# Down projections of two SwiGLU FFNs as Strassen pairs in a hybrid decoder layer

## Chip, core and metric

The kernel runs on one core of a Trainium2 chip. The metric is the device time of one execution in microseconds (us). Three executions of the kernel before took 1840.78, 1842.61 and 1845.76 us, median 1842.61. TensorE is called PE, VectorE DVE, ScalarE ACT, GpSimd POOL and SyncE SP; PEld is PE's loading of the stationary operand.

## Reference

One decoder layer on 256 tokens of width 2048, in float32. Two SwiGLU FFNs with inner width 5632 stand around a mixer; a gated per-layer embedding and a norm end it. Cut to what matters here:

```
def swiglu(x, w_gate, w_up, w_down):
    return (jax.nn.silu(x @ w_gate) * (x @ w_up)) @ w_down

h = h + 0.5 * swiglu(rms_norm(h, norm_ffn1[i]), w1_gate[i], w1_up[i], w1_down[i])
z = rms_norm(h, norm_mix[i]) @ w_in[i]
...            # s5 state space group, gMLP group, norms
h = h + y @ w_out[i]
h = h + 0.5 * swiglu(rms_norm(h, norm_ffn2[i]), w2_gate[i], w2_up[i], w2_down[i])
gate = jax.nn.sigmoid(rms_norm(h, norm_ple[i]) @ w_ple_gate[i])
h = h + gate * (p[i] @ w_ple_proj[i])
```

## The kernel before

**Three passes.** Every product keeps float32 accuracy by splitting each operand into a rounded high part and a rest: wh by ACT (L201) and wl by DVE (L202) for the weights, and the same for the 128x128 stationary blocks of activations. Each product is three matmuls of 512 columns: high times wh, high times wl, low times wh (L207 to L209).

**One stream.** The planner writes a list of steps, and `stream` runs it as one sequence of *subs*. A load brings 4 k rows of 512 columns of a weight (1 MB) into one of four buffers, three of `raw` and one of `xraw`. A sub takes two of the four k rows: one split on ACT and one on DVE, then 12 matmuls (2 k rows, 2 token halves, 3 passes). At sub i the splits up to sub i + 3 have been issued (`LA_SPLIT` = 3, four buffers of wh and wl). What belongs to a finished group of products (its `post`) is a generator, resumed some subs later, as many as it yields. All engines take their instructions in the order in which the program writes them, so a post stands in DVE's and ACT's queues behind the splits already issued.

**FFN.** The 5632 inner columns are 11 blocks c of 512. Gate and up of a block are 16 k rows each, 4 steps. In the second FFN blocks 1 to 10 are a `Pair`: gate and up run side by side, and the first of the four steps ("SNNN") is in Strassen's form: seven products P1, Q5, P2, P6, Q4, P7, P3 of 6 matmuls each, 42 instead of 48, with DVE sums s1 to s4 of the weights (L165) and sums of the transposed h made once (`sums_of_h`). P1, Q5, P6 and P7 have banks of PSUM of their own (`aux`), the others go straight into the four result banks C0 to C3 (`acc`); `aux_post` adds the own banks up afterwards. An ordinary step N has 4 subs, two of each weight.

**Turning g.** The product g = silu(gate) * up of a block is needed with its inner columns on partitions. `flip` transposes 32x32 squares on DVE (L492), writes the block to DRAM on POOL's queue and `fetch` reads it back in four transfers (L505); then ACT and DVE split it. In the first FFN all eleven blocks of g stay in SBUF as high and low parts (`gTa`, `gTb`); in the second, blocks 0 to 4 are kept in DRAM until gate and up are through.

**Down.** Four groups n of 512 result columns, one after another, each over 44 k rows (11 steps). The post of group n adds half of the result to h (L626, two DVE operations), takes squares for the next norm on ACT (L323), and turns the block of h for the next stage: n = 0 to 2 by `flip`, n = 3 by PE transposes (L299).

The functions that the change touches follow.

Of the kernel before, what the change touches and what calls it, by code (L numbers as in the profile page):

```python
# [15 lines left out]
P = 128  # L16
# [5 lines left out]
NW = 512  # L22
# [26 lines left out]
def steps_of(which, c):  # L49

    return "SNNN" if which == 2 and c > 0 else None
# [15 lines left out]
class Pair:  # L67


    ORDER = ("P1", "Q5", "P2", "P6", "Q4", "P7", "P3")  # L70
    BANK = {"P2": "C0", "Q4": "C1", "P3": "C2"}

    def __init__(self, layer, gate, up, steps, post):
        self.layer, self.groups, self.steps, self.post = layer, (gate, up), steps, post
        gate.pair = up.pair = self
        self.banks = {}
# [15 lines left out]
class Layer:  # L92
# [38 lines left out]
    def stream(self):  # L131
        nc = self.nc
        subs, loads = [], []
# [14 lines left out]
        raws, split, sums = {}, {}, {}  # L148
        paired = [i for i, e in enumerate(loads) if e[0].pair]
        p0, p1 = paired[0], paired[-1]  # L150
        state = {"ld": 0, "sp": 0}

        def load(li):
# [3 lines left out]
            pool = self.pools["xraw"] if p0 <= li <= p1 and (li - p0) % 4 == 3 else self.raw_p  # L157
# [24 lines left out]
        def do_split():  # L182
# [4 lines left out]
            if li >= p0 and ahead < p1:  # L187
# [42 lines left out]
        for i in range(n):  # L230
            ahead = i + LA_SPLIT + 1
# [5 lines left out]
            if isinstance(g, Pair):  # L237
                wh, wl = split.pop(i)
                name = g.ORDER[s0]
                for j in range(2):  # L240
                    into(g.bank(name), self.act_S(name, k0, j), wh[:, j], wl[:, j])
# [83 lines left out]
    def h_to_T(self, n, gcol, flip):  # L325

        if flip:
# [11 lines left out]
            if gcol == 32:  # L339
                yield from self.sums_of_h(n, tr)  # L340
# [14 lines left out]
    def sums_of_h(self, n, tr):  # L355

        nc = self.nc
        if n == 0:
            self.S = [self.pools["qt"].tile([P, BW], F32R, tag="qt", name=f"S{x}") for x in "hl"]
        st = self.pools["yss"].tile([P, 1024], F32, tag="st", name="st")  # L360
        a = tr.rearrange("p (i t kk u) -> p t kk i u", i=4, t=2, kk=4)
        a11, a12, a21, a22 = (a[:, t, k:k + 2] for t in range(2) for k in (0, 2))
        s1, s2, s3, s4 = (st[:, 256 * m:256 * m + 256].rearrange("p (kk i u) -> p kk i u", kk=2, i=4) for m in range(4))
        for o, x, y, op in ((s1, a21, a22, ALU.subtract), (s2, s1, a11, ALU.subtract), (s3, a11, a21, ALU.subtract),
                            (s4, a12, s2, ALU.add)):
            nc.vector.tensor_tensor(out=o, in0=x, in1=y, op=op)
        sh, sl = (x[:, 512 * n:512 * n + 1024] for x in self.S)
        yield 1
        self.split_plain(st, sh, sl)

# [3 lines left out]
    def kernel(self):  # L374
# [24 lines left out]
        self.gsk = [dram.tile([P, 4 * 256], F32, name=f"gsk{c}") for c in range(self.KA[1])]  # L399
# [14 lines left out]
        self.open_g(1)  # L414
        self.open("gs", "gs")
# [49 lines left out]


    KA = 6, 5

    def open_g(self, which):
        n = self.KA[which - 1]  # L470
        self.open("gta", "gt")
        self.gT_a = [self.pools["gta"].tile([P, n, 4 * 256], F32R, name=f"gTa{x}") for x in "hl"]

    def open_gb(self, which):
        self.open("gtb", "gtb")
        n = 11 - self.KA[which - 1]
        self.gT_b = [self.pools["gtb"].tile([P, n, 4 * 256], F32R, name=f"gTb{x}") for x in "hl"]

    def gT_at(self, which, c):
        n = self.KA[which - 1]  # L480
        if c < n:
            return self.gT_a, c
        return self.gT_b, c - n
# [23 lines left out]
    def ffn_groups(self, which):  # L507
# [5 lines left out]
        def gate_post(c):  # L513
            def post(g):
                if which == 2 and c == 0:
                    self.close_mix()
                    self.open_gb(2)
                    self.open("gs", "gs")
                    self.open("sums", "sums", 3)
                    self.open("xraw", "xraw")  # L520
# [8 lines left out]
        def up_post(c):  # L529
            def post(g):  # L530
                gt = st.pop(c)
                if which == 1 and c == 6:
                    self.close("wrk")
                    self.open_gb(1)
# [3 lines left out]
                yield from turn(c, gt)  # L538
            return post

        def split_g(c, tr):
            (th, tl), k = self.gT_at(which, c)
            self.split_plain(tr.rearrange("p (i b u) -> p b i u", i=4, b=8),
                             th[:, k, :].rearrange("p (b i u) -> p b i u", b=8, i=4),
                             tl[:, k, :].rearrange("p (b i u) -> p b i u", b=8, i=4))

        def turn(c, gt):
            if which == 2 and c < self.KA[1]:
                self.flip(gt, c)
                return  # L550
            tr = self.flip(gt)
            if which == 1 or c < 10:
                yield 6
                split_g(c, tr)
                return

            for x in ("xraw", "sums", "gs", "qt"):
                self.close(x)
            self.open_g(2)
            self.open("land", "land")  # L560
            land = self.pools["land"].tile([P, 4 * 256], F32, name="land")
            self.fetch(self.gsk[0], land)
            yield 6
            split_g(c, tr)
            split_g(0, land)
            self.fetch(self.gsk[1], tr)
            self.fetch(self.gsk[2], land)
            yield 4
            split_g(1, tr)
            self.fetch(self.gsk[3], tr)  # L570
            yield 1
            split_g(2, land)
# [766 lines left out]
```

## Time and profile before

| what | value |
|---|---|
| median of three executions | 1842.61 us |
| profiled execution | 1842.27 us, its span 1840.3 us |
| PE busy | 1827.1 us, 8452 matmuls |
| DVE busy, ACT busy | 1266.1 us, 891.9 us |
| splits of weights on DVE (L202) | 639 operations, 782.1 us |
| DMA | 405.11 MB, mean 220 GB/s |

A row of the timeline gives the start and the duration of an instruction in us, its engine, line, operation, output and inputs, and in brackets how long the engine stood idle before it and what released it. A matmul's duration is longer than the distance to the next one, since matmuls overlap; the distance between starts is what counts. The same holds, by less, for DVE operations that follow each other closely ("x2" in a row: two of them, with the time of both). A row by form gives count, busy time in all and the mean in ns of one operation.

### The profile page before, as it was taken

How to read it: one execution, taken by the hardware profiler on the slowest of the kernel's cores; microseconds unless marked ns; L12 is line 12 of the kernel's file. 1: busy time of each engine (PE TensorE's matmuls, PEld its weight loads, DVE VectorE, ACT ScalarE, POOL GpSimd, SP SyncE). 2: the span in 40 equal slices, each digit the busy share in tenths (PEclk: the TensorE clock that was granted, in tenths of full speed). 3: DMA queues.
4: the chain of work that ended last, by engine and by line, in shares of the span. 5: the costliest groups of instructions: out<-in, count | busy, mean ns of one | idle time of the engine just before them, and what ended most of it. 6: DMA issues, size and time to landing. Idle time of an engine off the chain costs nothing.

```text
span 1840.3 us, 22012 instructions
## 1 busy us (share of the span) xinstructions
PE 1827.1 (99%) x8452; PEld 1513.8 (82%) x8452; DVE 1266.1 (69%) x1701; ACT 891.9 (48%) x1054; POOL 132.3 (7%) x208
## 2 busy tenths in 40 slices
PE   9999999999999999999999999999999999999998
PEld 7888888888888888888888888888888888888887
DVE  6788886555545554688877678888888856455565
ACT  7444444444444444445446645555555545444454
POOL 1000000000000000022200000000000012000000
PEclk9999999999999999999999999999999999999999
DMA  8667777666666655566545665555666667566553
GB/s 329 225 243 264 241 262 252 225 211 224 223 208 209 223 211 195 223 246 223 181 177 189 225 235 199 195 216 197 232 235 226 222 217 258 197 222 212 193 203 136
DMA packets 72617, 405.11 MB, mean 220 GB/s; under 512 B 10176, under 2 KB 15552, under 8 KB 29888
## 3 DMA queue, kind: packets, MB, share of 16 engines
q1 hardware_dynamic: 62000, 371.67, 56.5%
q0 software_dynamic: 10080, 31.47, 5.7%
q8 instruction: 66, 1.08, 0.2%
q10 hardware_dynamic: 432, 0.57, 0.1%
q14 instruction: 39, 0.32, 0.0%
HBM read 376.28 MB, written 27.26 MB: 219 GB/s over the span
## 4 chain that ended last, share of the span: by engine, by line
PE 94%; DMA 2%; DVE 2%; issue 1%; ACT 1%; POOL 0%; SPq 0%; POOLq 0%; DVEq 0%; ACTq 0%
PE acc L207 23%; PE acc L209 23%; PE acc L208 23%; PE C L207 7%; PE C L209 7%; PE C L208 7%; DMA tr<-gsc 1%; PE P L208 1%; PE y L968 1%; PE P L209 1%; PE P L207 1%; DMA raw<-in_w_gate 1%; PE tr L299 1%; PE v L921 0%; DVE wl L202 0%
## 5 line engine op out<-in xcount | busy, mean ns | idle before, releaser
L202 DVE TENSOR_TENSOR wl<-raw,wh 128x1024 fp32r<-128x1024 f32 (+1 forms) x639 | 782.1, 1234 | 483.9 <-ACT wh L201 481.7
L201 ACT ACTIVATE wh<-raw 128x1024 fp32r<-128x1024 f32 (+1 forms) x639 | 674.4, 1058 | 709.4 <-PE acc L209 536.3
L207 PE MATMUL acc<-wh,hTh 128*128 128x512 f32 (+1 forms) x1104 | 432.0, 391 | 0.2 <-ACT wh L201 0.2
L208 PE MATMUL acc<-wl,hTh 128*128 128x512 f32 (+1 forms) x1104 | 429.3, 389 | 1.5 <-DVE wl L202 1.5
L209 PE MATMUL acc<-wh,hTl 128*128 128x512 f32 (+1 forms) x1104 | 429.2, 389 | 0.0
L208 PEld LDWEIGHTS acc<-wl,hTh 128*128 128x128 f32 x1104 | 207.4, 188 | 44.9 <-DVE wl L202 3.0
L207 PEld LDWEIGHTS acc<-wh,hTh 128*128 128x128 f32 x1104 | 207.3, 188 | 43.3 <-ACT wh L201 0.6
L209 PEld LDWEIGHTS acc<-wh,hTl 128*128 128x128 f32 x1104 | 207.3, 188 | 42.9
L207 PE MATMUL C<-wh,hTh 128*128 128x512 f32 x520 | 202.5, 389 | 0.0
L209 PE MATMUL C<-wh,hTl 128*128 128x512 f32 x520 | 202.5, 389 | 0.0
L208 PE MATMUL C<-wl,hTh 128*128 128x512 f32 x520 | 202.3, 389 | 0.0
L207 PE MATMUL acc<-wh,gTbh 128*128 128x512 f32 x352 | 137.1, 389 | 0.6 <-ACT gTbh L303 0.6
L209 PE MATMUL acc<-wh,gTbl 128*128 128x512 f32 x352 | 137.0, 389 | 0.5 <-DVE gTbl L304 0.5
L208 PE MATMUL acc<-wl,gTbh 128*128 128x512 f32 x352 | 136.9, 389 | 0.0
L207 PE MATMUL acc<-wh,gTah 128*128 128x512 f32 x352 | 136.9, 389 | 0.0
L208 PE MATMUL acc<-wl,gTah 128*128 128x512 f32 x352 | 136.9, 389 | 0.0
L209 PE MATMUL acc<-wh,gTal 128*128 128x512 f32 x352 | 136.9, 389 | 0.0
L209 PEld LDWEIGHTS C<-wh,hTl 128*128 128x128 f32 x520 | 97.6, 188 | 20.5
L208 PEld LDWEIGHTS C<-wl,hTh 128*128 128x128 f32 x520 | 97.6, 188 | 20.5
L207 PEld LDWEIGHTS C<-wh,hTh 128*128 128x128 f32 x520 | 97.6, 188 | 20.3
L498 POOL DMA_DIRECT2D gsc<-tr x25 | 14.2, 569 | 927.5 <-DVE tr L492 927.5
L207 PEld LDWEIGHTS acc<-wh,gTbh 128*128 128x128 f32 x352 | 66.1, 188 | 14.7 <-ACT gTbh L303 1.0
(288 smaller groups left out, 1841.4 us busy)
## 6 DMA issues: line engine op xcount, KB each, us to landing
raw<-in_w_up SPq DMA_DIRECT2D x88, 1024.0 KB, 5.8
raw<-in_w_down SPq DMA_DIRECT2D x88, 1024.0 KB, 4.8
raw<-in_w_gate SPq DMA_DIRECT2D x86, 1024.0 KB, 4.9
raw<-in_w_in SPq DMA_DIRECT2D x24, 1024.0 KB, 4.8
raw<-in_w_out SPq DMA_DIRECT2D x16, 1024.0 KB, 4.8
raw<-in_w_ple_gate SPq DMA_DIRECT2D x16, 1024.0 KB, 4.8
gsc<-tr POOLq DMA_DIRECT2D x25, 512.0 KB, 3.2
tr<-gsc POOLq DMA_DIRECT2D x100, 128.0 KB, 5.5
```

The lines of the kernel that those rows point to most:

```text
L201: nc.scalar.activation(out=wh[:, 0:nk, :], in_=src, func=AF.Copy)
L202: nc.vector.tensor_tensor(out=wl[:, 0:nk, :], in0=src, in1=wh[:, 0:nk, :].bitcast(F32), op=ALU.subtract)
L207: nc.tensor.matmul(o, a[0], wh, start=first, stop=False)
L208: nc.tensor.matmul(o, a[0], wl, start=False, stop=False)
L209: nc.tensor.matmul(o, a[1], wh, start=False, stop=last)
L299: self.nc.tensor.transpose(ps[:, i * P:(i + 1) * P], b, self.ident)
L498: nc.gpsimd.dma_start(out=sc, in_=tr)
L968: nc.tensor.matmul(ps[:, 64 * i:64 * i + 64], R[ri][:, i, :], qt[:, f0:f0 + 64], start=False, stop=(a == 1 and ri == 1))
```

## The change

- The four down groups become two pairs (columns 0 to 1023 and 1024 to 2047). Each pair goes over the 11 blocks of g with the steps `DOWN = "NSNNSNNSNNN"`, so 3 of 11 are in Strassen's form. The own banks are added up by `Pair.post` (the former `aux_post`), and `Pair.finish` adds that to each result bank before the post goes on.
- g of all eleven blocks, in both FFNs, is written to DRAM (`gsk`) and not fetched at once. In the down products `fetch(i)` brings block i into one of two `land` buffers, and `split_g(i)` splits it into one of three `stat` buffers one step ahead; for an S step it makes the four sums of that block and splits them too. As there are two pairs, each block is fetched and split twice per FFN. These calls stand in the plan as "do" entries at the start of each step.
- Blocks 8, 9 and 10 of the first FFN become gate/up pairs "SNNN"; the sums of the transposed h for them are made at block 6 (`sums_of_hT`).
- In both FFNs two more buffers of wh and wl (`ex`) let the splits run five subs ahead instead of three.
- Block n = 2 of h is turned by PE transposes, as n = 3 was; block n = 1 is turned six subs later than its group's end.

```diff
-    return "SNNN" if which == 2 and c > 0 else None
+    return "SNNN" if c > (7 if which == 1 else 0) else None
+DOWN = "NSNNSNNSNNN"
...
+    def finish(self, g, t):
+        i = self.groups.index(g)
+        x = self.rest[i][t]
+        self.layer.nc.vector.tensor_tensor(out=x, in0=g.ps[t], in1=x, op=ALU.subtract if i and t else ALU.add)
+        return x
...
+            if e[0] == "do":
+                at.setdefault(len(subs), []).append(e[1])
+                continue
...
-                wh = self.wh_p.tile([P, KS, NW], F32R, tag="wh", name="wh")
-                wl = self.wl_p.tile([P, KS, NW], F32R, tag="wl", name="wl")
+                ps = self.wh_p, self.wl_p
+                home[i] = self.ex_on > 0 and sum(not home[j] for j in split if j in home) > LA_SPLIT
+                if home[i]:
+                    ps = (self.pools["ex"],) * 2
+                wh = ps[0].tile([P, KS, NW], F32R, tag="wh", name="wh")
+                wl = ps[1].tile([P, KS, NW], F32R, tag="wl", name="wl")
...
-            ahead = i + LA_SPLIT + 1
+            for f in at.pop(i, ()):
+                f()
+            ahead = i + LA_SPLIT + 1 + self.ex_on
...
+        def fetch(i):
+            if i < 22:
+                land[i] = self.pools["land"].tile([P, 4 * 256], F32, tag="land", name="land")
+                self.fetch(self.gsk[i % 11], land[i])
+        def split_g(i):
+            if i == 22:
+                return
+            tr = land.pop(i)
+            stat[i] = [self.pools["stat"].tile([P, 4 * 256], F32R, tag=x, name=x) for x in ("gTh", "gTl")]
+            self.split_plain(tr.rearrange("p (i b u) -> p b i u", i=4, b=8),
+                             *(x.rearrange("p (b i u) -> p b i u", b=8, i=4) for x in stat[i]))
+            if DOWN[i % 11] == "S":
+                ss[i] = [self.pools["ss"].tile([P, 4 * 256], F32R, tag=x, name=x) for x in ("gSh", "gSl")]
+                st = self.pools["sums"].tile([P, 4 * 256], F32, tag="sum", name="st")
+                self.sums_of_T(tr.rearrange("p (i t kk u) -> p t kk i u", i=4, t=2, kk=4), st, *ss[i])
+        def at_step(i):
+            def f():
...
+                split_g(i + 1)
+                fetch(i + 3)
+            return f
...
+            for j in range(11):
+                self.plan += [("do", at_step(11 * p + j))] + pair.plan(j)
...
+        def down_post(n, pair):
             def post(g):
                 for t in range(2):
+                    x = pair.finish(g, t)
                     hs = self.h[:, t, n * NW:(n + 1) * NW]
                     self.nc.vector.scalar_tensor_tensor(
-                        out=hs, in0=g.ps[t], scalar=0.5, in1=hs, op0=ALU.mult, op1=ALU.add)
+                        out=hs, in0=x, scalar=0.5, in1=hs, op0=ALU.mult, op1=ALU.add)
...
-                yield from self.h_to_T(n, 16 if which == 1 else 48, n < 3)
+                if n == 1:
+                    yield 6
+                yield from self.h_to_T(n, 16 if which == 1 else 48, n < 2)
```

Three places of the order that the prediction speaks of, all in the first FFN (the second has the same). Place A is DVE's queue at the first S step after gate/up; g and z, y are the gate and up results, C their banks, s the weight sums, st the sums of a block of g. Before, the down products follow the last block of gate/up like this:

```order
L492 STREAM_TRANSPOSE tr<-g_3926 128x4x4x32
L492 STREAM_TRANSPOSE tr<-g_3927 128x4x4x32
L202 TENSOR_TENSOR wl<-raw,wh 128x1024 x6
L304 TENSOR_TENSOR gTbl<-tr,gTbh 128x1024
L202 TENSOR_TENSOR wl<-raw,wh 128x1024 x16
```

Now the end of the last gate/up pair and the first S step of the down products share the stretch:

```order
L248 TENSOR_TENSOR wl<-s_4142,wh 128x1024
L107 TENSOR_TENSOR y<-C_3914,y 128x512
L107 TENSOR_TENSOR z<-C_3973,z 128x512
L207 TENSOR_TENSOR s_4204<-s_4182,raw 128x1024
L248 TENSOR_TENSOR wl<-raw,wh 128x1024
L207 TENSOR_TENSOR s_4224<-raw 128x1024
L248 TENSOR_TENSOR wl<-s_4182,wh 128x1024
L603 SCALAR_TENSOR_TENSOR g_3942<-y,r_95,g_3942 128x512
L603 SCALAR_TENSOR_TENSOR g_3943<-z,r_95,g_3943 128x512
L542 STREAM_TRANSPOSE tr<-g_3942 128x4x4x32
L542 STREAM_TRANSPOSE tr<-g_3943 128x4x4x32
L248 TENSOR_TENSOR wl<-s_4204,wh 128x1024
```

The finish of the pair (L107), its products (L603) and transposes (L542) now stand between the splits of the S step's factors.

Place B is DVE's queue where the second half of the down products begins; before, that is between the groups n = 1 and n = 2:

```order
L626 SCALAR_TENSOR_TENSOR h<-acc_4472,h 128x512
L626 SCALAR_TENSOR_TENSOR h<-acc_4473,h 128x512
L492 STREAM_TRANSPOSE tr<-h 128x4x4x32 x2
L202 TENSOR_TENSOR wl<-raw,wh 128x1024 x6
L338 TENSOR_TENSOR hTl<-tr,hTh 128x4x128 x2
```

Now, from the end of the first pair on to the first S step's Q5:

```order
L107 TENSOR_TENSOR y<-C_4230,y 128x512
L675 SCALAR_TENSOR_TENSOR h<-y,h 128x512
L107 TENSOR_TENSOR z<-C_4231,z 128x512
L675 SCALAR_TENSOR_TENSOR h<-z,h 128x512
L352 TENSOR_TENSOR gTl<-land,gTh 128x1024
L411 TENSOR_TENSOR st<-land 128x256
L411 TENSOR_TENSOR st<-st,land 128x256
L411 TENSOR_TENSOR st<-land 128x256
L411 TENSOR_TENSOR st<-land,st 128x256
L352 TENSOR_TENSOR gSl<-st,gSh 128x1024
L207 TENSOR_TENSOR s_5145<-s_5101,raw 128x1024
L248 TENSOR_TENSOR wl<-s_5101,wh 128x1024
```

Two operations per result block became four, and the split of g with its sums stands behind them, ahead of the second factor's split.

Place C is DVE's queue at the end of the FFN, where h of the last block is made for PE's transposes. Before:

```order
L202 TENSOR_TENSOR wl<-raw,wh 128x1024 x16
L626 SCALAR_TENSOR_TENSOR h<-acc_5266,h 128x512
L626 SCALAR_TENSOR_TENSOR h<-acc_5267,h 128x512
L288 TENSOR_TENSOR rs<-ssq_102 128x2
L290 TENSOR_TENSOR rs<-rs,ssq_102 128x2 x2
```

Now:

```order
L248 TENSOR_TENSOR wl<-raw,wh 128x1024
L365 SCALAR_TENSOR_TENSOR hTl<-tr,gcol,hTh 128x256 x2
L248 TENSOR_TENSOR wl<-raw,wh 128x1024
L365 SCALAR_TENSOR_TENSOR hTl<-tr,gcol,hTh 128x256 x2
L107 TENSOR_TENSOR y<-C_5191,y 128x512
L675 SCALAR_TENSOR_TENSOR h<-y,h 128x512
L107 TENSOR_TENSOR z<-C_5192,z 128x512
L675 SCALAR_TENSOR_TENSOR h<-z,h 128x512
```

The operations that make h stand behind those that split the turned block n = 2 (hTl), which wait for ACT and for PE's transposes of that block.

## Rows read from the trace of the kernel before

**Rows 1.** Page, busy time, share of the span and instructions of each engine

```profile
PE 1827.1 (99%) x8452; PEld 1513.8 (82%) x8452; DVE 1266.1 (69%) x1701; ACT 891.9 (48%) x1054; POOL 132.3 (7%) x208
```

**Rows 2.** Waits of PE: line, what it waited for, us in total, times, longest

```profile
PE acc L208 <- DVE wl L202: 1.5, 3, 0.8
...
PE acc L207 <- ACT gTbh L303: 0.6, 1, 0.6
PE acc L209 <- DVE gTbl L304: 0.5, 1, 0.5
...
PE P L208 <- DVE wl L202: 0.2, 1, 0.2
```

**Rows 3.** Window of one gate/up pair in the second FFN

```profile
core 0: us, PE busy (x) PEld busy (x) DVE busy (x) ACT busy (x) POOL busy (x), PEclk, DMA share, GB/s
1110.52:1152.95 42.43, 42.43 (x187) 34.85 (x187) 34.31 (x36) 21.89 (x22) 0.55 (x1) 1.00 0.59 210
```

**Rows 4.** Timeline of PE: plain subs, then one Strassen step (42 matmuls from 1108.99)

```profile
1105.59 0.39 PE L207 MATMUL C<-wh,hTh 128*128 128x512 f32 x1
...
1108.31 0.39 PE L207 MATMUL C<-wh,hTh 128*128 128x512 f32 x1
...
1108.99 0.39 PE L207 MATMUL P<-wh,hTh 128*128 128x512 f32 x1
...
1118.75 0.40 PE L207 MATMUL C<-wh,hTh 128*128 128x512 f32 x1
```

**Rows 5.** Chain of waits: start us, us, what; FFN ends

```profile
739.09 0.44 PE tr L299 x4
...
1510.01 7.48 DMA tr<-gsc
```

**Rows 6.** Groups of instructions by form

```profile
L202 DVE TENSOR_TENSOR wl<-raw,wh 128x1024 fp32r<-128x1024 f32 x637 | 780.7, 1236 | 481.5 <-ACT wh L201 479.3
...
L165 DVE TENSOR_TENSOR s<-raw 128x1024 f32<-128x1024 f32 x20 | 24.3, 1216 | 0.0
L323 ACT ACTIVATE junk<-h 128x512 f32<-128x512 f32 x38 | 24.0, 631 | 31.4 <-DVE h L626 15.1 <-DVE h L1109 8.9 <-DVE h L1214 6.9
...
L303 ACT ACTIVATE gTah<-tr 128x1024 fp32r<-128x1024 f32 x8 | 8.4, 1054 | 7.4 <-DMA tr<-gsc 7.4
...
L323 ACT ACTIVATION_READ_ACCUMULATOR junk<-h 128x1 f32 x38 | 7.1, 186 | 0.0
```

**Rows 7.** Timeline of DVE around one Strassen step, operations close together

```profile
1109.07 1.22 DVE L202 TENSOR_TENSOR wl<-raw,wh 128x1024 fp32r<-128x1024 f32 x1 [0.62 <-ACT wh L201]
1110.21 1.22 DVE L165 TENSOR_TENSOR s<-raw 128x1024 f32<-128x1024 f32 x1
...
1113.62 0.68 DVE L605 TENSOR_TENSOR y<-C,y 128x512 f32<-128x512 f32 x1
1114.22 0.68 DVE L605 TENSOR_TENSOR z<-C,z 128x512 f32<-128x512 f32 x1
...
1119.36 0.74 DVE L609 SCALAR_TENSOR_TENSOR g<-y,r,g 128x512 f32<-128x512 f32 x1
...
1120.68 1.29 DVE L492 STREAM_TRANSPOSE tr<-g 128x512 f32<-128x512 f32 x2
1121.90 2.31 DVE L202 TENSOR_TENSOR wl<-raw,wh 128x1024 fp32r<-128x1024 f32 x2
...
1124.14 0.68 DVE L588 TENSOR_TENSOR g<-P,g 128x512 f32<-128x512 f32 x1
1124.85 0.69 DVE L589 TENSOR_TENSOR y<-Q,g 128x512 f32<-128x512 f32 x1
```

**Rows 8.** Timeline of DVE, four sums of a stationary, first and next operation

```profile
1006.83 0.42 DVE L366 TENSOR_TENSOR st<-tr 128x256 f32<-128x256 f32 x1
...
1008.30 0.87 DVE L317 SCALAR_TENSOR_TENSOR hTl<-tr,gcol,hTh 128x256 fp32r<-128x256 f32 x2
```

**Rows 9.** Page, DMA issues: KB each, median us from issue to landing

```profile
raw<-in_w_down SPq DMA_DIRECT2D x88, 1024.0 KB, 4.8
...
tr<-gsc POOLq DMA_DIRECT2D x100, 128.0 KB, 5.5
```

More of the change, by code (lines that the diff above doesn't have):

```diff
@@ L147, in stream @@
         n_tail = sum(sb[0] is tail for sb in subs)
-        raws, split, sums = {}, {}, {}
-        paired = [i for i, e in enumerate(loads) if e[0].pair]
-        p0, p1 = paired[0], paired[-1]
+        raws, split, sums, home = {}, {}, {}, {}
+        run = {}
+        i = 0
+        while i < len(loads):
+            j = i
+            while j < len(loads) and loads[j][0].pair:
+                j += 1
+            for x in range(i, j):
+                run[x] = i, j - 1
+            i = j + 1
         state = {"ld": 0, "sp": 0}
@@ L156, in load @@
             g, k0, nk = loads[li]
-            pool = self.pools["xraw"] if p0 <= li <= p1 and (li - p0) % 4 == 3 else self.raw_p
+            pool = self.pools["xraw"] if li in run and (li - run[li][0]) % 4 == 3 else self.raw_p
             t = pool.tile([P, KL, NW], F32, tag="raw", name="raw")
@@ L186, in do_split @@
             ahead = li + (3 if isinstance(g, Pair) and s0 > 2 else 2)
-            if li >= p0 and ahead < p1:
+            if li in run and ahead < run[li][1]:
                 ahead += 1
@@ L547, in turn @@
[L547 to L572, printed above, removed]
-            self.fetch(self.gsk[4], land)
-            yield 3
-            split_g(3, tr)
-            yield 1
-            split_g(4, land)
@@ L579, in pair_of @@
[L579 to L592 removed]
+                self.flip(gt, c)
@@ L602, in up_end @@
                 yield 1
-                for t, op in enumerate((ALU.add, ALU.subtract)):
-                    x = m["u"][t]
-                    self.nc.vector.tensor_tensor(out=x, in0=g.ps[t], in1=x, op=op)
+                us = [pair.finish(g, t) for t in range(2)]
                 yield 2
+                gt = pair.rest[0]
                 for t in range(2):
-                    x = m["g"][t]
-                    self.nc.vector.scalar_tensor_tensor(out=x, in0=m["u"][t], scalar=r[:, t:t + 1], in1=x,
+                    self.nc.vector.scalar_tensor_tensor(out=gt[t], in0=us[t], scalar=r[:, t:t + 1], in1=gt[t],
@@ L610, in up_end @@
                                                         op0=ALU.mult, op1=ALU.mult)
-                yield from turn(c, m["g"])
+                self.flip(gt, c)
             gate.post, up.post = gate_end, up_end
-            pair = Pair(self, gate, up, steps_of(which, c), aux_post)
-            for j, x in enumerate(pair.steps):
-                self.plan += [("S", pair, 4 * j)] if x == "S" else [(gate, 4 * j, 4), (up, 4 * j, 4)]
-        def act_g(k, t):
-            x, c = self.gT_at(which, k // 4)
+            pair = Pair(self, gate, up, steps_of(which, c), self.act_S)
@@ L646, in ffn_groups @@
                 self.whole(up)
-        first = 0 if which == 1 else self.KA[1]
-        for n in range(4):
-            g = Group(wd, n * NW, 44, act_g, down_post(n))
-            self.plan += [(g, 4 * (c % 11), 4) for c in range(first, first + 11)]
+        for p in range(2):
+            down_pair(p)
     def vexp(self, pool, x, out):
@@ L1263, in final_post @@
             yield 1
-        tail = self.plan[-1][0]
-        last = tail.post
+        before = self.plan[-1][0]
+        last = before.post
         def last_post(g):
-            def both():
-                yield from last(g)
-                yield from prep()
-            return both()
-        tail.post = last_post
+            yield from last(g)
+            yield from prep()
+        before.post = last_post
         G = self.whole
```

150 lines of the change are left out of this document (86 added, 64 removed).

## Prediction

> **What bounds the kernel now.** I read the page's busy times first: TensorE (PE) is busy for 1827.1 of 1840.3 us [rows 1], at a granted clock of 1.00 where I looked [rows 3]. The list of PE's waits comes next, since a busy PE could still be held up: its named waits are few, the longest 0.8 us, and the two at the hand-over from the gate/up products to the down products of the second FFN make 1.1 us [rows 2]. So the time is the number of matmuls times their spacing, and whatever the change takes off PE is gained unless PE is made to wait for it. Spacing comes from PE's timeline. Twelve matmuls of a plain half step (one *sub*: two k rows, two token halves, three passes) take 1108.31 - 1105.59 = 2.72 us, 0.2267 each. The 42 of a Strassen step go from 1108.99 to 1118.75, 9.76 us, 0.2324 each [rows 4]. One period of a gate/up pair "SNNN" (one S step, three plain ones) is 42.43 us [rows 3].
>
> **What it removes.** A plain pair of four steps would be 192 matmuls of 0.2267, 43.53 us; the pair with one S step takes 42.43, so one S step is worth 1.10 us. The change adds 12 of them in the down products (3 of 11 steps, two pairs, two FFNs) and 3 in the first FFN: 15 x 1.10 = -16.5 us. The other end is six matmuls at the plain spacing, 1.36 each, -20.4; I take the period, which is a whole pair as it ran. The 1.1 us of waits at the second FFN's hand-over go, as g is fetched two steps ahead there [rows 2]. Sum -17.6.
>
> That an S step runs at 0.2324 instead of 0.2267 a matmul is a row [rows 4]. The Trainium skill ("SBUF — State Buffer", SBUF: two separate sides) says that PE, ScalarE and VectorE's own port pair never wait on one another at SBUF; by that rule the S matmuls would keep the plain spacing where no operand is late, the 15 steps would be worth 20.4 us and the forecast below would be 3.9 lower, 1842.6. This trace does not bear it out for S steps, and the sum goes by the row.
>
> **What it adds on PE.** Column block n = 2 of h was turned by VectorE (DVE) and DRAM in both FFNs and is now turned on PE: 8 transposes per FFN, 0.44 us per four [rows 5], +1.8 us in all.
>
> **What it adds beside PE, and where that ends late.** The extra work goes to DVE. One after the other its 128x1024 operations start 1.14 us apart, 128x512 ones 0.60 (PSUM operand), 0.66 (scalar form), 0.61 (transposes), and 0.71 where each needs the one before [rows 7]. The four 256-wide sums of a stationary take 1.47 us [rows 8]. ScalarE (ACT) takes 1.06 us for a split, 0.63 + 0.19 for a square [rows 6].
>
> An ordinary S step of the down products follows two plain ones. Count from the start of the plain step ahead of it (t = 0), four subs of 2.72, so the S products start at 10.88 and each factor lasts 9.76 / 7 = 1.39. A factor's second matmul needs wl, so wl is due 0.23 after the factor's start: Q5 12.5, P2 13.9, P6 15.3, Q4 16.7, P7 18.1. DVE is done with P1 at -0.2 at the earliest, as the sixth buffer comes free only when PE ends a sub. Then come in order gTl 1.14, the sums 1.47, the wait for ACT's gSh 1.15, gSl 1.23, three sums and three wl (6 x 1.14 = 6.84), Q4, the next step's gTl and P7 (3 x 1.14 = 3.42): 15.25, so P7 is ready at 15.05 against 18.1. Slack 3.1 us, no wait. Over three steps DVE has some 29 us of work in 31.5.
>
> At three places per FFN something else stands in that stretch; the rows of the order show each.
>
> *Place A, the first S step after gate/up.* Ahead of P1's split ACT has the two Silu that wait for two DVE sums (P1 ready 1.7 later). Behind Q5 come two sums 1.2, behind P6 two products 1.32 and two transposes 1.22: 5.4 more, less 3.1 of slack: wait 2.4, most of it at Q4 and P7.
>
> *Place B, the first S step of the second down pair.* Before P1 DVE has the four operations of the first block's end (0.71 + 0.62 twice, 2.7) and two transposes 1.22, and may only begin them when PE has ended that block at t = -5.2; P1 comes 2.65 later than in the ordinary case. Four more operations for the second block stand before gTl: 2.7. ACT's two squares of that block (the second can start only after the last of the four) hold ACT's gTh back, and DVE idles 2.0. Two hTl later add 1.22. Together 8.6 less 3.1: wait 5.5, at Q5, P2, P6 and P7.
>
> *Place C, the end of the FFN.* The transposes of block 3 stand on PE one sub behind the last product, and need h. Before, two DVE operations led to h and PE did not wait. Now four operations of 2.7 in all, and they are queued behind the hTl of block 2, which wait for ACT, which waits for PE's transposes: DVE starts them at about 3.0 after the last product's end and h is ready at 5.7, where PE arrives at 3.6: wait 2.1.
>
> Twice each: 2 x (2.4 + 5.5 + 2.1) = +20.0 us. Bounds: nothing (PE waited at most 0.8 anywhere [rows 2]), or the whole extra work without the slack, 2 x (5.4 + 8.6 + 2.7) = 33. I take the count in order, as DVE and ACT take their instructions strictly in it.
>
> The fetch of g costs nothing: 0.5 MB in four transfers, at worst 7.48 us of landing [rows 5] plus four issues, asked for two steps (20 us) ahead into two buffers; its cover is the step in between, and without it ACT would wait in order and each us late would be a us of S slack. The weights' loads stay four buffers deep: a load lands in 4.8 us [rows 9] and is asked for six splits ahead, 6.8 us when DVE runs at its fastest, so catching up after A and B does not outrun them. POOL's queue holds a flip's write ahead of a fetch at A and B; the fetch behind it is due 12 us later. Splits five ahead cost buffers only, and take from the S steps the little they waited before (0.2 us in one, rows 2; not counted). Writing g of eleven blocks to DRAM without fetching it back at once frees ACT and DVE in gate/up, where nothing waits.
>
> **Sum.** -17.6 + 1.8 + 20.0 = +4.2 against the profiled execution's 1842.27 (span 1840.3 and 2.0 around it): 1846.5. The median of the three runs, 1842.61, lies 0.3 above that execution, too little to shift it.
>
> **Rivals.** (1) *DVE hides it.* If the five-deep buffer carries DVE over A and B, only C and scraps of the waits stay, 5 us or less: 1842.3 - 17.6 + 1.8 + 0 to 5 = 1826.5 to 1831.5. For it: ten S steps started in the second FFN with splits only three ahead and DVE busy for 34.31 of 42.43 us [rows 3], and waited hardly at all [rows 2]. Against it: none of them had a stationary to split and sum within the same stretch. Chance 0.20.
>
> (2) *DVE stays behind, slower.* With 29 of 31.5 us in the three-step cycle DVE is 93% booked. If its operations run nearer to their means, 1.236 and 1.216 us [rows 6], it is 30.9, 98%: then the backlog of A and B is not worked off before the next S step, and the remaining eight ones wait some 1.5 us each as well. It decides from about 31 us of DVE work per cycle. Price +12: 1858. The Trainium skill ("VectorE: DVE Perf Modes", The DRAIN you can't avoid) has the next DVE operation start only when the pipe is empty; by that A and B alone grow by a us each and the time by 4. Rows 7 disagree: the next operation starts 0.08 before the end of the one before. Chance 0.20.
>
> (3) *It does not do it.* The order has 25 chains of s1 to s4 instead of 10 and 90 fewer long matmuls, so this is out.
>
> **How the numbers follow.** My forecast, waits of 15 to 27 us, holds 0.60: 1841 to 1853. Rival 1 holds 0.20, rival 2 0.20. A measurement of this kernel tells about 0.3%, 5.5 us, from no change: 1837.1 to 1848.1. Of the forecast's 0.60 I put 0.43 within and 0.17 above; so faster 0.20, same 0.43, slower 0.37. The range leaves out the lower half of rival 1 and the upper half of rival 2: 1830 to 1857.
>
> **What would show it.** Right: PE's waits rise from 6 to about 25 us, named wl at the factors of S steps, longest about 2 us and clustered at four S steps (the first of each down pair), and two waits of about 2 us of the transposes for h; the other 8 down S steps without wait; the matmuls fewer by 90; S steps at 9.7 to 9.8 us where nothing waits. Wrong: waits under 8 us in all (rival 1), waits at every S step of the down products or loads of weights among what ACT waits for there (rival 2), S steps that take much less or more than 9.76.

## The result, and the profile after

The changed kernel took 1862.41 us (median of 1861.41 to 1863.68), the kernel before 1843.12 beside it: ratio 1.0105, 95% interval 1.0087 to 1.0122. It is slower by 1%, 16 us above the forecast and 5 above the range. The profiled execution (1863.68) has a span of 1862.0, 21.7 more than that of before.

The page's busy times, to be held against [rows 1]:

```profile
PE 1823.2 (98%) x8378; PEld 1504.9 (81%) x8378; DVE 1473.3 (79%) x1956; ACT 967.3 (52%) x1138; POOL 175.0 (9%) x286
```

PE has 74 recorded matmuls fewer (90 fewer in the S steps, 16 transposes more) and is busy for 4 us less, yet the span grew: PE waits. The upper part of PE's list of waits (us in total, times, longest), to be held against [rows 2]:

```profile
PE C L253 <- DVE y L107: 7.3, 2, 3.6
PE P L254 <- DVE wl L248: 6.1, 8, 1.6
PE C L254 <- DVE wl L248: 4.3, 4, 1.6
PE Q L254 <- DVE wl L248: 3.0, 2, 1.5
PE tr L347 <- DVE h L675: 2.8, 4, 1.0
PE acc L253 <- ACT wh L247: 2.3, 1, 2.3
PE acc L254 <- DVE wl L248: 1.8, 2, 1.0
```

The first row is the largest, and a wait for result banks was in no term of the sum. It stands where the down products begin (PE's timeline, first FFN):

```profile
497.73 0.39 PE L255 MATMUL C<-wh,gTl 128*128 128x512 f32 x1
501.75 0.77 PE L253 MATMUL C<-wh,gTh 128*128 128x512 f32 x1 [3.63 <-DVE y L107]
502.32 0.63 PE L254 MATMUL C<-wl,gTh 128*128 128x512 f32 x1
502.74 0.63 PE L255 MATMUL C<-wh,gTl 128*128 128x512 f32 x1
```

The first half of the first down step has gone into C0 and C1. The second half wants the two banks in which the up group of the last gate/up pair lies until DVE has read it. After the wait the starts are 0.43 apart, not 0.2267 as in [rows 4]. The windows of that place tell why (columns as in [rows 3]; the granted clock stands behind the five engines):

```profile
497.73:501.75 4.02, 0.39 (x2) 0.03 (x1) 4.02 (x5) 2.69 (x3) 1.37 (x3) 0.91 0.49 130
501.75:507.44 5.69, 5.69 (x14) 4.43 (x15) 5.69 (x7) 0.14 (x1) 0.00 (x0) 0.50 0.30 94
```

For 5.7 us PE ran at a granted clock of 0.50 (1.2 GHz, called half clock below) after it had stood. DVE's timeline ahead of it names what the banks waited for:

```profile
495.96 0.42 DVE L411 TENSOR_TENSOR st<-land,st 128x256 f32<-128x256 f32 x1
497.51 1.23 DVE L352 TENSOR_TENSOR gSl<-st,gSh 128x1024 fp32r<-128x1024 f32 x1 [1.13 <-ACT gSh L351]
498.65 1.22 DVE L207 TENSOR_TENSOR s<-s,raw 128x1024 f32<-128x1024 f32 x1
499.78 1.22 DVE L248 TENSOR_TENSOR wl<-s,wh 128x1024 fp32r<-128x1024 f32 x1
500.92 0.69 DVE L107 TENSOR_TENSOR y<-C,y 128x512 f32<-128x512 f32 x1
501.52 0.69 DVE L107 TENSOR_TENSOR z<-C,z 128x512 f32<-128x512 f32 x1
```

The two sums that free the banks (L107) stand in DVE's queue behind the whole split of g for the S step and behind a weight sum and a split of weights.

A further place is the start of the second FFN. PE stops twice there. Its timeline, that of ACT and, from the windows, the granted clock behind the stops:

```profile
1046.80 0.49 PE L253 MATMUL acc<-wh,hTh 128*128 128x512 f32 x1 [2.27 <-ACT wh L247]
1048.31 0.80 PE L254 MATMUL acc<-wl,hTh 128*128 128x512 f32 x1 [1.01 <-DVE wl L248]
```

```profile
1040.56 1.15 ACT L384 ACTIVATE hTh<-tr 128x512 fp32r<-128x512 f32 x2
1044.02 1.06 ACT L351 ACTIVATE Sh<-st 128x1024 fp32r<-128x1024 f32 x1 [2.31 <-DVE st L411]
1044.98 0.82 ACT L362 ACTIVATE hTh<-tr,gcol 128x256 fp32r<-128x256 f32 x2
1045.69 3.89 ACT L247 ACTIVATE wh<-raw 128x1024 fp32r<-128x1024 f32 x4
```

```profile
1049.00:1053.60 4.60, 4.60 (x13) 3.58 (x12) 2.66 (x3) 0.78 (x2) 0.00 (x0) 0.50 0.96 340
```

ACT stands at Sh (split of the sums of the turned h) until DVE has made the sums, and the weights' splits that PE needs are queued behind it. Before, a `yield 1` lay between sums and split; the new `sums_of_T` has none.

And S steps themselves, when nothing waits: 42 matmuls from the first to the next step's first.

```profile
510.19 0.39 PE L253 MATMUL P<-wh,gTh 128*128 128x512 f32 x1
...
519.71 0.39 PE L253 MATMUL C<-wh,gTh 128*128 128x512 f32 x1
```

That is 9.52 us, 0.2267 a matmul, not the 9.76 of [rows 4]; 7 of the 12 down S steps ran so, and those of gate/up in 9.69.

Waits by place, worked out from the starts of PE's matmuls (each distance above 0.25, less 0.227; the half-clock matmuls counted in), first and second FFN:

| place | forecast | measured |
|---|---|---|
| A, end of gate/up | 2.4 + 2.4, at Q4 and P7 | 6.7 + 5.5, at the banks |
| B, first S step of the second pair | 5.5 + 5.5 | 5.4 + 5.4 |
| other down S steps | 0 | 4.6 + 4.0 |
| C, end of the FFN | 2.1 + 2.1 | 1.9 + 1.9 |
| start of the second FFN | no change | 7.8, before 1.2 |
| second FFN's hand-over, before | 1.1 goes | 1.7 went |

Sum: 43.2 of waits now, 2.9 then, +40.3. S steps: 12 x (10.88 - 9.52) + 3 x (10.88 - 9.69) = 19.9, and ten older ones at 9.69 instead of 9.76, 0.7. With 1.8 for transposes: 40.3 - 20.6 + 1.8 = 21.5, against 21.7 measured. The waits in the first 30 us of the kernel, 2.4 before and 1.3 now, are left out.

### The profile page after: what moved, and what is told of

It is laid out like the page before. It is cut to its first block, busy times and chain, and to the rows that moved or that the text cites. A ratio compares the mean times of both kernels' runs of the same rounds, so it can differ in the third digit from the quotient of the medians.

```text
span 1862.0 us, 22502 instructions
## 1 busy us (share of the span) xinstructions
PE 1823.2 (98%) x8378; PEld 1504.9 (81%) x8378; DVE 1473.3 (79%) x1956; ACT 967.3 (52%) x1138; POOL 175.0 (9%) x286
## 4 chain that ended last, share of the span: by engine, by line
PE 84%; DVE 6%; DMA 4%; issue 3%; ACT 2%; POOL 1%; SPq 0%; DVEq 0%; POOLq 0%; ACTq 0%
PE C L253 13%; PE C L254 13%; PE C L255 13%; PE acc L253 12%; PE acc L254 12%; PE acc L255 12%; DVE wl L248 2%; PE P L254 2%; PE P L255 2%; PE P L253 2%; DMA gsc<-tr 1%; DMA tr<-gsc 1%; DMA raw<-in_w_down 1%; DVE gTl L352 1%; PE tr L347 1%
## 5 line engine op out<-in xcount | busy, mean ns | idle before, releaser
L253 PE MATMUL acc<-wh,hTh 128*128 128x512 f32 x912 | 358.8, 393 | 3.1 <-ACT wh L247 2.3
L254 PE MATMUL acc<-wl,hTh 128*128 128x512 f32 x912 | 355.9, 390 | 1.8 <-DVE wl L248 1.8
L255 PE MATMUL acc<-wh,hTl 128*128 128x512 f32 x912 | 355.8, 390 | 0.0
L253 PE MATMUL C<-wh,gTh 128*128 128x512 f32 x560 | 220.6, 394 | 7.5 <-DVE y L107 7.3
L254 PE MATMUL C<-wl,gTh 128*128 128x512 f32 x560 | 220.7, 394 | 4.3 <-DVE wl L248 4.3
L255 PE MATMUL C<-wh,gTl 128*128 128x512 f32 x560 | 220.2, 393 | 0.0
L247 ACT ACTIVATE wh<-s 128x1024 fp32r<-128x1024 f32 x100 | 105.7, 1057 | 86.1 <-PE C L255 53.3
L248 DVE TENSOR_TENSOR wl<-s,wh 128x1024 fp32r<-128x1024 f32 x100 | 121.2, 1222 | 30.5 <-ACT wh L247 30.0
L253 PEld LDWEIGHTS C<-wh,gTh 128*128 128x128 f32 x560 | 106.4, 190 | 30.9 <-ACT wh L247 8.7
L254 PEld LDWEIGHTS C<-wl,gTh 128*128 128x128 f32 x560 | 106.4, 190 | 27.9 <-DVE wl L248 5.9
```

Of the source, the lines that this page charges most:

```text
L247: nc.scalar.activation(out=wh[:, 0:nk, :], in_=src, func=AF.Copy)
L248: nc.vector.tensor_tensor(out=wl[:, 0:nk, :], in0=src, in1=wh[:, 0:nk, :].bitcast(F32), op=ALU.subtract)
L253: nc.tensor.matmul(o, a[0], wh, start=first, stop=False)
L254: nc.tensor.matmul(o, a[0], wl, start=False, stop=False)
L255: nc.tensor.matmul(o, a[1], wh, start=False, stop=last)
```

## Experiments

All times are medians, with the ratio to the kernel before run beside them. "Down" is the length of a down stage, from its first to its last matmul with g in PE's timeline: before 239.1 and 240.8 (first, second FFN), changed 248.6 and 246.5.

**e1: free the banks first.** In `up_end` the first `yield 1` is left out:

```diff
             def up_end(g):
-                yield 1
                 us = [pair.finish(g, t) for t in range(2)]
```

> The changed kernel, but the sums that read the two result banks of the up group of a gate/up pair are issued at once at the group's end instead of one sub later, so they stand in VectorE's queue ahead of the split of the next block of g and its four sums. Theory 1 (the wait at the hand-over from gate/up to down is PE waiting for two of its four result banks, and the half clock of 3 to 6 us behind it comes from that wait): the two waits of 3.79 us net and the half-clock matmuls behind them (2.7 and 1.5 us) go, 11.8 us in all: 1850.6 if nothing takes their place, up to 1855.4 if the predicted 2.4 us at Q4 and P7 of the first S step now show twice. Granted clock 1.00 in the 12 us after the hand-over. Theory 2 (the half clock has another reason than the wait): only 7.6 us go, 1854.8, and the stretch at 0.50 stays. Theory 3 (VectorE is simply behind here, whatever the order): the wait moves to the S step's wl, 1860 to 1863.

1863.14 us, ratio 1.0110 (1.0097 to 1.0123): no gain. The bank wait is gone from the list, and so is the half clock; the windows of that place in e1 show 1.00:

```profile
493.20:508.16 14.96, 14.96 (x67) 12.39 (x66) 13.76 (x18) 6.98 (x8) 2.34 (x5) 1.00 0.35 113
508.16:514.00 5.84, 4.01 (x17) 2.69 (x16) 5.84 (x6) 5.08 (x6) 1.89 (x4) 1.00 0.46 182
```

Theory 1 held for the banks. PE now waited 1.6 us at P6 and 0.5 at P7 of the first S step: 2.1, close to the 2.4 of the prediction, though it had put them at Q4 and P7. But the later S steps of the first pair wait as well, which had not; from e1's list of PE's waits:

```profile
PE P L254 <- DVE wl L248: 13.4, 19, 1.6
```

In the changed kernel DVE and the loads went on while PE stood. Without that stop DVE has to stand for its loads itself; in the stretch from 513 to 612 us, first in e1, then in the changed kernel:

```profile
DVE s L207 <- DMA raw<-in_w_down: 8.3, 2, 4.4
```

```profile
DVE s L207 <- DMA raw<-in_w_down: 2.6, 1, 2.6
```

So the time is that of theory 3, but not its reason: DVE was late because it waited, not because it had too much work.

**e2: sums and split apart.** In `h_to_T`:

```diff
-                self.sums_of_T(trv, st, *self.S_of(n))
+                self.sums_of_T(trv, st)
+                S = self.S_of(n)
+                yield 1
+                self.split_plain(st, *S)
```

> The changed kernel, but at the end of the mixer the split of the sums of the turned h (Sh, Sl) is issued one sub after the sums themselves, as in the kernel before. Theory 1 (PE's waits of 2.66 and 1.51 us at the start of the second FFN, and the 4.6 us at half clock behind them, come from ScalarE standing at Sh until the sums are done, with the weights' splits queued behind): about 6 us less, 1856.4; the stretch from the end of the out projection to the second FFN's down products falls from 476.3 to about 470. Theory 2 (they come from the later landing of the turned block of h): 0 to 1 us less, 1861.5 to 1862.4, same waits.

1856.79 us, 1.0073 (1.0060 to 1.0086). The stretch from the out projection to the second FFN's down products fell from 476.3 to 469.7 us (before 470.1). Theory 1, to the size.

**e3: the place of the S steps.**

```diff
-DOWN = "NSNNSNNSNNN"
+DOWN = "NNSNNSNNSNN"
```

> The changed kernel with the three Strassen steps of each down pair one step later, NNSNNSNNSNN instead of NSNNSNNSNNN. Theory 1 (what was lost is the meeting of the first S step's work with the end of the pair ahead of it): the bank waits at the hand-over (with half clock 11.8 us) and the waits at the first S step of the second pair (2 x 4.9 us) go, and the later S steps keep what they have or less: 1862.4 - 11.8 - 9.8 = 1840.8, up to 1846 if the turned blocks of h now meet the S step. Theory 2 (S steps in the down products wait because VectorE has too much to do over three steps): the waits move with the S steps, 1855 or more, and VectorE shows no idle time before them.

1855.84 us (1850.04 to 1859.27), 1.0068 (1.0054 to 1.0082): 6.6 less, not the 16 to 22 of theory 1. Theory 2 has the time but not the reason: DVE stood idle for down loads, 22.6 us in all. In the profile (its fastest execution) the bank wait and three quarters of B are gone, but the second S step of the second pair waits more: ACT stood 8.27 us at its gSh.

**e4: no S step in the down products.**

```diff
-DOWN = "NSNNSNNSNNN"
+DOWN = "N" * 11
...
     def finish(self, g, t):
+        if not self.rest:
+            return g.ps[t]
```

> The changed kernel with no Strassen step in the down products (the pairs, the reading of g from DRAM twice and the splits five ahead stay). Price of the 12 steps if they did not wait: + 12 x 1.10 to 1.20 = 13.2 to 14.4 us. Theory 1 (the waits in the down products come from S steps beside the ends of pairs and blocks): their waits go, 11.8 + 9.8 + 7.9 = 29.5 us: 1846 to 1847.5. Theory 2 (pairs and the reading of g cost by themselves, S steps little): the waits stay in the main, 1865 or more. What is then left over the kernel before, beside 1.8 us of transposes, is the second FFN's start (6.2 us) and the FFN ends (1.7 twice), less 3.3 for the three pairs of the first FFN: 1842.3 + 1.8 + 6.2 + 3.4 - 3.3 - 1.1 = 1849.

1844.72 us, 1.0009 (1.0000 to 1.0018): theory 1, a little below its range. Both down stages take 239.6 and have no wait. So pairs, the reading of g from DRAM twice and the splits ahead cost nothing to speak of; the S steps made the loss, and an S step that did not wait is worth 239.6/22 - 9.52 = 1.37.

**e5, e6: loads or splits ahead.** e6 opens `ex` with one buffer and sets `ex_on = 1`; e5 does that and gives `xraw` a second buffer:

```diff
-        self.open("ex", "ex", 2)
-        self.open("xraw", "xraw")
-        self.ex_on = 2
+        self.open("ex", "ex", 1)
+        self.open("xraw", "xraw", 2)
+        self.ex_on = 1
...
-            pool = self.pools["xraw"] if li in run and (li - run[li][0]) % 4 == 3 else self.raw_p
+            pool = self.pools["xraw"] if li in run and (li - run[li][0]) % 5 >= 3 else self.raw_p
```

> The changed kernel with five load buffers in the FFNs instead of four (a second xraw) and, to make room, one extra buffer of wh and wl instead of two, so splits run four ahead. To be read beside e6_four_ahead, which has the splits four ahead and four load buffers. Theory 1 (the later S steps of a down pair wait because their weights are asked for too late: once VectorE is behind, a load buffer comes free late, the load lands late, and VectorE stands at the first sum of the S step with the split of g behind it): VectorE's 14.8 us of waits of the weight sums for loads fall under 5, and the kernel is 6 to 10 us faster than e6_four_ahead. Theory 2 (VectorE has too much work, the loads only follow it): same time as e6_four_ahead within 3 us.

> The changed kernel with one extra buffer of wh and wl instead of two: splits run four subs ahead instead of five. Theory 1 (what holds the S steps is the loads or the order of the queues, not how far the splits run ahead): within 3 us of 1862.4. Theory 2 (VectorE is carried over the crowded places by the lead of its splits, 2.72 us a sub): 1.4 to 2.7 us more of wait at each first S step of a pair, four of them: 1868 to 1873.

e5 1865.62, 1.0128 (1.0113 to 1.0143); e6 1865.40, 1.0122 (1.0105 to 1.0139). Equal: theory 2 of e5, and theory 1 of e6 at its edge. In both, DVE's waits for down loads (14.8 us in the changed kernel) are gone from the list, with four load buffers as with five, and S steps wait as before. So the fifth buffer had nothing left to take, and the waits for loads alone do not explain the S steps. The fifth sub ahead is worth at most 3 us, which the two intervals do not tell from nothing, and not 6 to 11.

**e7: weight sums just in time.** In `factor`, s1, s2, s4 and s3 are made at m = 1, 2, 3, 4 instead of 0 to 3.

```diff
-            if m == 0:
+            if m == 1:
                 add(li, "s1", g0, u0)
...
```

> The changed kernel with each of the four sums of weights of an S step issued one factor later, just ahead of the factor that needs it. The first sum needs the second of the step's two loads; it then stands in VectorE's queue behind the split of the next block of g and its four sums instead of ahead of them. Theory 1 (the late second load holds the split of g, ScalarE's gSh behind it and so the whole S step): the later S steps of the second pair lose most of their wait (7.9 us in both FFNs) and the first ones some: 1853 to 1858. Theory 2 (VectorE's work as a whole is the bound): no change, 1860 to 1864, or more, since ScalarE then waits for each sum.

1871.14 us, 1.0154 (1.0139 to 1.0170): 9 slower than the changed kernel, on the side of theory 2 and above its range. ACT now waits for each sum, in gate/up too, and the stop at the banks has grown from 4.0 to 5.3 us:

```profile
ACT wh L247 <- DVE s L207: 102.1, 58, 2.9
```

**e8: gSh half a step after its sums.** In `split_g` only the sums are made; a new "do" entry in the middle of the step splits them:

```diff
-                self.sums_of_T(tr.rearrange("p (i t kk u) -> p t kk i u", i=4, t=2, kk=4), st, *ss[i])
+                self.sums_of_T(tr.rearrange("p (i t kk u) -> p t kk i u", i=4, t=2, kk=4), st)
+                ready[i] = st
...
+        def mid_step(i):
+            def f():
+                if i + 1 in ready:
+                    self.split_plain(ready.pop(i + 1), *ss[i + 1])
+            return f
...
-                self.plan += [("do", at_step(11 * p + j))] + pair.plan(j)
+                steps = pair.plan(j)
+                self.plan += [("do", at_step(11 * p + j)), steps[0], ("do", mid_step(11 * p + j))] + steps[1:]
```

> The changed kernel with one edit: the split of the sums of a block of g (gSh on ScalarE, gSl on VectorE) is issued half a step after the sums, not at once. Theory 1 (ScalarE stands in order at gSh until VectorE has made the sums, 52.9 us in all, while the splits of weights behind it wait and VectorE waits for them; that is what makes the S steps late): the waits at the S steps of the second pair (2 x 4.9 and 7.9 us) fall by half or more, 1850 to 1855; ScalarE's idle time at gSh under 15 us. Theory 2 (the position of the S step next to the end of the pair before is what counts): 1858 to 1862.

1857.01 us, 1.0077 (1.0062 to 1.0092), between the two theories. ACT's idle time at gSh fell from 52.9 (the row below, of the changed kernel) to 10.5 us:

```profile
ACT gSh L351 <- DVE st L411: 52.9, 12, 7.0
```

PE now waits for gS itself:

```profile
PE Q L255 <- DVE gSl L352: 7.6, 4, 2.5
PE Q L253 <- ACT gSh L351: 4.2, 2, 2.6
```

The largest of these waits stand at Q5 of the first two S steps of the second pair. There, half a step later is too late.

**c1, c2: edits together.** c1 is e1 + e2 + e3 + e8, c2 is c1 without e8.

> Four edits of order together: the finish of the up group at once (e1), the split of the mixer's sums one sub later (e2), the Strassen steps one step later (e3), and the split of the sums of a block of g (gSh, gSl) half a step after the sums, so ScalarE does not stand at gSh while the splits of weights wait behind it (52.9 us of such idle time in the changed kernel). From e3's 1855.8: less 6 for e2: 1850. Theory 1 (the rest of the waits comes from ScalarE's and VectorE's queues standing at g's split): another 4 to 8 us less, 1842 to 1846. Theory 2 (the loads of weights land late whatever the order): 1849 to 1851, with waits for loads as in e3.

> Three of the four edits of c1: the finish of the up group at once, the mixer's split of the sums one sub later, the Strassen steps one step later; the split of the sums of g at once, as in the changed kernel. Theory 1 (ScalarE standing at gSh): the edit left out is worth 8 to 16 us here: 1843 to 1850. Theory 2 (position alone): 1834 to 1838, as c1.

c1 1834.38 us, 0.9951 (0.9934 to 0.9968): faster than both kernels and below both theories. Alone the four edits come to 16.9 us less, together to 28.0. c2 1844.47 (1840.42 to 1853.73), 1.0021 (1.0005 to 1.0038): theory 1. By the medians e8 is worth 10 here, 5 alone; c2's executions lie 13 us apart, so the 10 is rough. The longest wait left in c1, 3.3 us net in the second FFN with 2 us of half clock, comes from DVE standing at the first weight sum, whose load is late, with the split of g behind it:

```profile
1649.35 1.23 DVE L207 TENSOR_TENSOR s<-raw 128x1024 f32<-128x1024 f32 x1 [5.96 <-DMA raw<-in_w_down]
```

**k1: g earlier.** c1, with g of an S step split in the middle of the step before last:

```diff
         def mid_step(i):
             def f():
                 if i + 1 in ready:
                     self.split_plain(ready.pop(i + 1), *ss[i + 1])
+                if i + 2 < 22 and DOWN[(i + 2) % 11] == "S":
+                    split_g(i + 2)
...
-                split_g(i + 1)
+                if i + 1 not in stat:
+                    split_g(i + 1)
```

> c1 with the split of the block of g for an S step and its four sums another half step earlier, in the middle of the step before last, so that they stand ahead of the S step's first weight sum, which waited up to 6 us for its load in c1. Theory 1 (that order held the second S step of the second pair, 3.5 us with 2 us at half clock in the second FFN, 1.3 and less in the first): 3 to 7 us less than c1's 1834.4: 1828 to 1831. Theory 2 (the load is late whatever stands behind the sum): 1833 to 1836.

1828.54 us, 0.9926 (0.9910 to 0.9943). Theory 1. The down stages are 232.0 and 233.1 us, with 2.0 us of waits left.

**k2: two operations at the group's end.** k1, and the sums of `Pair.post` go into h at once (`Pair.finish` then hands back the bank itself, as in e4):

```diff
+            def pre():
+                yield from Pair.post(pair)
+                yield 1
+                for i in range(2):
+                    for t in range(2):
+                        hs = self.h[:, t, (2 * p + i) * NW:(2 * p + i + 1) * NW]
+                        self.nc.vector.scalar_tensor_tensor(out=hs, in0=pair.rest[i][t], scalar=-0.5 if i and t else 0.5,
+                                                            in1=hs, op0=ALU.mult, op1=ALU.add)
+                pair.rest = []
+            pair.post = pre
```

> k1, and what Pair.post has added up is added to h as soon as it is there, after the last S step, so that the end of a down group is two VectorE operations, as in the kernel before, not four. The 1.66 us for which PE's transposes wait for h at the end of each FFN go, 3.3 us, and the end of the first pair is lighter by 2.7 us of VectorE's work: 1824.5 to 1828; if the eight moved operations only make other S steps late, 1829 to 1833.

1826.13 us, 0.9910 (0.9896 to 0.9925), the fastest and as expected. PE's waits in all:

```profile
PE Q L257 <- DVE gSl L354: 2.2, 1, 2.2
PE acc L256 <- DVE wl L250: 1.8, 2, 1.1
PE warm L475 <- POOL mhalf L450: 1.4, 1, 1.4
PE tr L349 <- DVE h L702: 0.3, 2, 0.2
PE acc L255 <- ACT wh L249: 0.2, 1, 0.2
```

Place C is gone (2.8 to 0.3).

**k4: place or order.** k1 without e3:

> k1 without the move of the Strassen steps: the order NSNNSNNSNNN of the changed kernel, with g of an S step split and summed in the middle of the step before last (for the very first S step, which has only one down step ahead of it, at the start of the step before, as in the changed kernel). Theory 1 (the order of the queues was the cause, the place of the S step little): 1829 to 1834. Theory 2 (the place counts: the first S step needs two plain steps between it and the end of the pair before, which brings 5.4 us of work at the hand-over and 8.6 at the second pair): 2 to 6 us of waits at each first S step come back, 1838 to 1848.

1850.44 us, 1.0042 (1.0028 to 1.0056). Theory 2, above its range. The four kernels side by side, us ("orders" are e1, e2, e8 and k1's edit):

| | S at 1, 4, 7 | S at 2, 5, 8 |
|---|---|---|
| orders as changed | 1862.4 | 1855.8 |
| orders mended | 1850.4 | 1828.5 |

Of the 12.0 in the first column 5.6 are e2's. The place is worth 6.6 without the orders and 21.9 with them. k4's two down stages hold 23.1 us of waits, k1's 2.0. The longest of them is in k4's second FFN, second pair: ACT stands 8.9 us in front of the scaling of the turned block n = 1 of h, and PE waits 5.4 behind it.

```profile
1655.45 1.70 ACT L380 ACTIVATE tr<-tr,gcol 128x256 f32<-128x256 f32 x4 [8.91 <-DMA land<-gsk]
```

The row names a fetch of g (land), which had been issued behind the block's own fetch. POOL's timeline shows the block's way, written at 1634.0 and fetched only when the write has landed:

```profile
1634.01 0.56 POOL L552 DMA_DIRECT2D gsc<-tr  x1 [3.58 <-DVE tr L546]
1643.33 2.18 POOL L559 DMA_DIRECT2D tr<-gsc  x4 [8.77 <-DMA gsc<-tr]
```

In k1, with the S steps one later, ACT takes the block at 1634, among plain steps. What the other waits of k4 come from was not followed.

## Why the prediction was wrong

**The ground held.** PE bounds the kernel, S steps pay, and the waits beside them decide. Place B (10.8 us, forecast 11.0) and place C (3.8, forecast 4.2) came out as counted, and B at the factors that the prediction names: PE waited at Q5, P2, P6 and P7, and DVE stood 1.80 us (counted 2.0) ahead of gTl:

```profile
621.67 1.23 DVE L352 TENSOR_TENSOR gTl<-land,gTh 128x1024 fp32r<-128x1024 f32 x1 [1.80 <-ACT gTh L351]
```

PE's list of waits rose from 4.4 to 30.0 us (forecast: from 6 to about 25). That PE waited "at most 0.8 anywhere" overlooked 1.4 us for POOL at the kernel's start, which touches no term.

**Place A failed.** The prediction saw in the order that the two sums which read the last up banks stand behind Q5's split, and asked only who waits for wl at the S step. PE's own plain step ahead of it needed the banks: 12.2 us instead of 4.8, of which 4.6 are slow matmuls behind the stop. e1 shows both: with the banks free the forecast wait came (2.1, forecast 2.4), at P6 and P7, and no half clock.

**That the other 8 down S steps do not wait failed: 8.6 us.** The slack of 3.1 us per S step was counted on DVE alone. It left out that ACT's queue is also in order, so the weights' splits stand behind a gSh whose sums are not ready; that the block n = 1 of h returns in the second pair's second S step, where DVE stood 1.3 and 2.2 us for it; and that, once DVE catches up, the loads do come late. How the 8.6 us divide among the three no run tells. The sentence that "catching up after A and B does not outrun them" was wrong. It took 4.8 us for a load [rows 9]; a down load now landed in 7.4:

```profile
raw<-in_w_down SPq DMA_DIRECT2D x88, 1024.0 KB, 7.4
```

That alone costs nothing: e4, without S steps, has 7.4 too and no wait. But ahead of the second S step of the second pair DVE stood for the load and ACT behind DVE (timelines of DVE, then ACT):

```profile
652.63 1.23 DVE L207 TENSOR_TENSOR s<-raw 128x1024 f32<-128x1024 f32 x1 [1.95 <-DMA raw<-in_w_down]
```

```profile
657.62 1.06 ACT L351 ACTIVATE gSh<-st 128x1024 fp32r<-128x1024 f32 x1 [6.16 <-DVE st L411]
```

What stands in order behind the load counts: k1, which moves the split of g ahead of the sum that waits for it, gained 5.8 us over c1.

**The start of the second FFN was left out: +6.6 us.** One removed line of the diff, a `yield 1` of `sums_of_h`, was not followed into ACT's queue. e2 gave 5.6 back.

**The gain of an S step was taken too small.** 1.10 was read from a period in which S steps ran at 9.76. In the down products they ran at 9.52, the prediction's other end of 1.36: 19.9 us instead of 16.5. That "this trace does not bear it out for S steps" rested on gate/up S steps with splits three ahead; with five ahead these took 9.69. Here the Trainium skill ("SBUF — State Buffer", SBUF: two separate sides) agrees with the down S steps' 0.2267; what holds those of gate/up at 9.69 no run tells.

**Rival 2 was nearest in time (1858), not in cause.** It had DVE's operations at their longer means, 98% booked, and S steps waiting for that. One of its signs came: ACT waited 22.1 us for down loads, and not at all before. But in the last cycle of the first pair of the changed kernel, where PE never waits, DVE (third engine) is busy for 27.39 of 33.00 us:

```profile
579.00:612.00 33.00, 33.00 (x148) 27.31 (x147) 27.39 (x29) 17.12 (x19) 7.98 (x15) 1.00 0.98 298
```

k1 runs the same operations, with the S steps one place later, and has 2.0 us of waits in its down stages. DVE had the time; the order in which it and ACT were given the work lost it. That 1858 lies near the measured time is chance.

## What to carry to other kernels

When an order moves a PSUM reader back, ask not only who reads its result but which matmul wants the bank. In a kernel whose engines take their work in order, put no instruction that waits for another engine's fresh result, or for a load, ahead of work that is due sooner: the same operations cost 1862 us in one order and 1828 in another (k1). An experiment that takes out one wait in such a chain may gain nothing (e1) although the wait was real; test the edits together before dropping them.

## What the runs showed of the hardware

In several places PE came back at half clock after it had stood. In the changed kernel, after one stop of 4.0 us the window of 5.7 us behind it shows 0.50 (13 starts 0.43 apart); after two stops of 2.7 and 1.5 us in a row, 4.6 us at 0.50 (both windows shown above). Behind two stops of 0.6 and 2.1 us in a row came 3.0 us at 0.53, while place B, four stops of 1.0 to 2.0 us within 11 us with at least five matmuls between two of them, stayed at 1.00:

```profile
627.14:638.19 11.05, 6.73 (x26) 4.28 (x24) 11.05 (x12) 9.21 (x14) 0.89 (x2) 1.00 0.37 126
...
1678.48:1681.50 3.02, 3.02 (x7) 2.33 (x8) 3.02 (x3) 2.75 (x3) 0.00 (x0) 0.53 0.61 198
```

The length of a stop alone does not tell what follows. In e2's second FFN the same stop of 4.0 us at the banks was followed by 1.00, and in k2 a single stop of 2.6 us by 4.6 us at 0.65 (the stop, then the window behind it; e2, then k2):

```profile
1503.90:1507.92 4.02, 0.40 (x2) 0.02 (x1) 4.02 (x5) 2.70 (x3) 1.38 (x3) 1.00 0.50 130
1507.92:1513.00 5.08, 5.07 (x22) 4.21 (x23) 5.08 (x6) 2.00 (x2) 0.00 (x0) 1.00 0.22 56
```

```profile
1650.00:1652.60 2.60, 0.40 (x2) 0.00 (x0) 2.57 (x4) 2.00 (x2) 0.00 (x0) 1.00 0.49 87
1652.60:1657.20 4.60, 4.59 (x14) 3.62 (x15) 4.60 (x5) 3.27 (x4) 0.00 (x0) 0.65 0.53 215
```

So a stop can cost more than its own length: in the first FFN of the changed kernel the 4.0 us brought 2.9 more of slow matmuls. But the same stop does not always do so, and what decides it no run here tells. The half clock in the table of waits is that of the profiled execution.
